# Prompt attention of a hybrid decoder step: scores over all 128 rows, value products of two heads by turns, compressed keys in one block-diagonal tile

## The chip, the cores and the metric

One core of a Trainium2 chip runs the whole program. The metric is the device time of one execution in microseconds (us), the median of the runs shown. Below, PE is TensorE's matrix engine and PEld its weight loads, DVE is VectorE, ACT is ScalarE, POOL is GpSimd; PSUM is the memory that TensorE writes, in banks of 128 rows x 512 float32 values.

## What is computed

The reference is one step of a decoder with two layers, for a prompt of 512 tokens and 8 samples of one token each, which share all weights. A layer is a feed-forward half step, three mixers side by side (a state space model, sparse attention, a short convolution) that gates merge, and a second half step. The change concerns the prompt's part of the attention mixer. There are 8 query heads in 2 groups (the kv heads), 4 queries (g) for each kv head, 64 features per head. Three branches are added with gates:

```python
s_c = jnp.einsum('btkgd,bnkd->btkgn', qg, kc)           # 31 compressed keys
p_c = masked_softmax(s_c, (c_end[None, :] <= q_pos[:, None])[None, :, None, None, :])
o_c = jnp.einsum('btkgn,bnkd->btkgd', p_c.astype(vc.dtype), vc)
...
s_s = jnp.einsum('btkgd,btknsd->btkgns', qg, ks_sel)    # selected keys
...
s_w = jnp.einsum('btkgd,bwkd->btkgw', qg, kw)           # keys of the window
...
o = g[..., 0:1] * o_c + g[..., 1:2] * o_s + g[..., 2:3] * o_w
```

With 512 prompt tokens, there are 8 blocks to select from and 16 may be selected, and the window holds 512: the selected and the window branch are both full causal attention, with keys and values of their own.

## The kernel before

Everything runs feature-major, and products are kept near float32's accuracy: a float32 operand is split into two parts, a first one (float32r) and the rest, and a product is the sum of three (lines 239 to 241 for the large projections). After the projections of queries, keys and values, the cached rows are compressed (lines 705 to 770, with the prompt's own 31 compressed keys going along with the first sample), interleaved with the samples' attention (`samples`, four pairs). The last pair's attention then runs together with `prompt_attention`: `weave` emits the two streams by turns, by the cost in ns that each step yields. Within that the scheduler of the language may still move an instruction ahead of others on its engine. After it come the state space mixer, the convolution and the gates.

`prompt_attention` works on four query tiles t of 128 tokens. Each has one unit for the compressed keys (`pa_cmp`) and eight units `pa_head`, for 2 branches (br) and 4 heads g of a group; a unit handles both kv heads. With nk = 128 (t + 1) keys, a unit of `pa_head` does, for each kv, the scores, their maximum by rows (DVE, line 1053) and the exponential (ACT, line 1054) into P; then, for each kv, `flip` transposes P in pieces of 128 (PE, line 1062) and copies it out of PSUM to PT (kv = 0 by DVE, line 1066, kv = 1 by ACT, line 1064); then `values` multiplies (PE, line 1071) and accumulates into the bank y, kv = 0 in its partitions 0 to 63 and kv = 1 in 64 to 127, that is through the two column halves of PE. At a branch's last head, the gates over the sums are brought in by four products (line 1092), DVE and POOL.

A score is the sum of three products on PE:

```python
nc.tensor.matmul(S[:, :nk], Q[:, kv, g], self.ks[:, kv, br, :nk], start=True, stop=False, ...)       # 1050
nc.tensor.matmul(S[:, :nk], Q[r, 2, g], self.ks[r, kv, br, :nk], start=False, stop=False, ...)       # 1051
nc.tensor.matmul(S[:, ts], self.identb, self.causal, start=False, stop=True, ...)                    # 1052
```

`ks[:, kv]` holds the first part of kv's keys on its own 64 rows and the second part on the other 64 (`pa_keys`); `Q[:, kv]` holds the first part of the queries twice, so line 1050 gives first by first and first by second over all 128 rows. Line 1051 adds the queries' second part by the keys' first part, on the 64 rows r of kv alone. Line 1052 adds the causal mask. `pa_queries` (lines 959 to 966) makes Q for a tile, by four ACT copies and two DVE subtractions, in a buffer named raw.

The units are emitted as a pipeline of three, two halves i each: in half 0 the first score of unit n, the first step of unit n-1 and the last of unit n-2; in half 1 the second score of unit n and the second step of unit n-1. Before, the steps of a unit are: scores kv 0; scores kv 1; flip 0; values 0 with flip 1; values 1.

`pa_cmp` has the heads in two passes, one for each kv, on 64 rows: a mask product (line 1004) and four products of 32 columns (line 1007) with the compressed keys `kcp`, then maximum, exponential and sums for all eight heads, two transposes (line 1026) and four products with the values (line 1033). The tiles P and PT of `pa_head` take the names whi and wlo of the weights' buffers that they share, and a PSUM bank is always ps.

## Time and profile before

| | |
|---|---|
| runs, median (lowest to highest) | 3239.26 us (3226.91 to 3241.25), 3 runs |
| the profiled execution, span | 3260.5 us, 62256 instructions |
| busy over the span | PE 3183.1 us (98%), PEld 3011.0 (92%), DVE 1595.2 (49%), ACT 1121.7 (34%), POOL 534.0 (16%) |
| mean granted clock of TensorE | 0.978 of full |
| prompt attention, layer 0 and layer 1 | 678 to 846 us and 2299 to 2467 us, 168 us each |

The profiled execution has no other time than its span; it lies 21 us, 0.7%, above the median of the runs. The profile's busy times are averages over stages, and a matmul's end in it is modelled: a row's duration covers the matmul's way through the engine, so consecutive rows overlap. What a product costs where TensorE is never short of work is the distance from its start to the start of the next one. Some records are missing. An fp32 product leaves two records (two passes), an fp32r or bf16 product one.

### The profile page before, as it was taken

What the parts mean: (1) busy time and instruction counts of PE and PEld (TensorE: products, weight loads), DVE (VectorE), ACT (ScalarE), POOL (GpSimd) and SP (SyncE); (2) the same over time, 40 slices, a digit from 0 to 9 for tenths busy, and PEclk for the clock granted to TensorE, in tenths of its full rate; (3) what the DMA queues carried; (4) which work ended last, traced back from release to release, by engine and by line L of the source; (5) the groups of instructions that cost most, each with busy time, mean ns of one, the idle gap of its engine ahead of it and who ended that gap; (6) DMA issues with size and microseconds to landing.
All of it is one profiled execution on the core that took longest, in us unless ns stands there. A gap on an engine that the chain in (4) does not pass through costs nothing. (4 is left out here: it accounts for less than half of the span.)

```text
span 3260.5 us, 62256 instructions
## 1 busy us (share of the span) xinstructions
PE 3183.1 (98%) x25436; PEld 3011.0 (92%) x25436; DVE 1595.2 (49%) x3590; ACT 1121.7 (34%) x2226; POOL 534.0 (16%) x807
## 2 busy tenths in 40 slices
PE   9999999999999999999999999899999999999998
PEld 8999988776899999999999999887769999999998
DVE  7633446444555455333486334455446553553334
ACT  4332225444333333332233322344443343343322
POOL 3601111211001012001147012111210010120010
PEclk9999989988999999999999999999889999999999
DMA  4543244620444332322235323445205532322321
GB/s 151 212 153 117 96 140 130 196 65 21 135 131 118 96 99 78 99 83 98 74 121 166 110 82 107 138 134 173 74 13 143 143 109 87 98 91 91 102 84 63
DMA packets 358631, 360.19 MB, mean 110 GB/s; under 512 B 40068, under 2 KB 341668, under 8 KB 358216
## 3 DMA queue, kind: packets, MB, share of 16 engines
q1 hardware_dynamic: 342584, 333.58, 32.9%
q0 software_dynamic: 7440, 20.00, 2.1%
q8 instruction: 200, 3.28, 0.4%
q10 hardware_dynamic: 8320, 2.62, 0.4%
q14 instruction: 87, 0.71, 0.1%
HBM read 332.48 MB, written 36.28 MB: 113 GB/s over the span
## 5 line engine op out<-in xcount | busy, mean ns | idle before, releaser
L239 PE MATMUL ps<-xh,whi 128*128 128x264 f32 (+1 forms) x4448 | 1259.8, 286 | 21.3 <-ACT xh L322 5.7
L240 PE MATMUL ps<-xl,whi 128*128 128x264 f32 (+1 forms) x4448 | 1260.5, 285 | 2.3 <-DVE xl L323 2.0
L241 PE MATMUL ps<-xh,wlo 128*128 128x264 f32 (+1 forms) x4448 | 1256.0, 284 | 5.5 <-issue 2.8
L239 PEld LDWEIGHTS ps<-xh,whi 128*128 128x128 f32 x4448 | 838.0, 190 | 30.3 <-ACT xh L322 7.9
L229 DVE TENSOR_TENSOR wlo<-raw,whi 128x1024 fp32r<-128x1024 f32 (+3 forms) x432 | 497.4, 1154 | 736.5 <-ACT whi L228 733.4
L240 PEld LDWEIGHTS ps<-xl,whi 128*128 128x128 f32 x4448 | 840.9, 189 | 5.4 <-DVE xl L323 3.3
L241 PEld LDWEIGHTS ps<-xh,wlo 128*128 128x128 f32 x4448 | 840.4, 189 | 5.6 <-DVE wlo L229 3.8
L228 ACT ACTIVATE whi<-raw 128x1024 fp32r<-128x1024 f32 (+2 forms) x452 | 444.4, 988 | 886.4 <-PE ps L240 774.6
L240 PE MATMUL ps<-hl,whi 128*128 128x256 f32 (+1 forms) x1408 | 398.3, 283 | 0.0
L239 PE MATMUL ps<-hh,whi 128*128 128x256 f32 (+1 forms) x1408 | 398.2, 283 | 0.0
L241 PE MATMUL ps<-hh,wlo 128*128 128x256 f32 (+1 forms) x1408 | 398.1, 283 | 0.0
L241 PEld LDWEIGHTS ps<-hh,wlo 128*128 128x128 f32 x1408 | 265.3, 188 | 0.2
L239 PEld LDWEIGHTS ps<-hh,whi 128*128 128x128 f32 x1408 | 264.8, 188 | 0.3
L240 PEld LDWEIGHTS ps<-hl,whi 128*128 128x128 f32 x1408 | 264.8, 188 | 0.1
L260 POOL TENSOR_TENSOR xf<-xf,shift 128x264 f32<-128x264 f32 (+1 forms) x84 | 79.4, 982 | 1026.2 <-ACT shift L257 1026.2
L384 DVE TENSOR_TENSOR s<-s,ps 128x264 f32<-128x264 f32 (+1 forms) x176 | 74.3, 424 | 275.9 <-PE ps L241 275.6
L708 PE MATMUL ps<-xc,whi 128*128 128x256 f32 (+1 forms) x1024 | 167.9, 297 | 1.2 <-DVE xc L694 1.2
L385 ACT ACTIVATE hh<-s 128x264 fp32r<-128x264 f32 (+1 forms) x176 | 72.7, 415 | 245.0 <-DVE s L384 244.9
L708 PEld LDWEIGHTS ps<-xc,whi 128*128 128x128 f32 x1024 | 141.3, 191 | 16.7 <-issue 9.6
L1112 POOL DMA_INDIRECT sg<-in_selT_dram,idx x96 | 92.7, 966 | 295.8 <-PE ps L1247 261.8
L1053 DVE TENSOR_REDUCE pm<-ps 128x1 f32<-128x128 f32 (+3 forms) x128 | 62.1, 488 | 111.6 <-PE ps L1052 111.2
L382 ACT ACTIVATE s<-ps 128x264 f32<-128x264 f32 (+1 forms) x176 | 66.2, 378 | 128.4 <-PE ps L241 126.2
(469 smaller groups left out, 4449.0 us busy)
## 6 DMA issues: line engine op xcount, KB each, us to landing
raw<-in_ffn_w_gu_dram SPq DMA_DIRECT2D x86, 1024.0 KB
raw<-in_w_in_dram SPq DMA_DIRECT2D x38, 1024.0 KB
raw<-in_ffn_w_down_dram SPq DMA_DIRECT2D x32, 1024.0 KB
sg<-in_selT_dram SPq DMA_DIRECT2D x160, 128.0 KB
cx<-in_cmpT_dram SPq DMA_DIRECT2D x128, 128.0 KB
raw<-in_cmpT_dram SPq DMA_DIRECT2D x128, 128.0 KB
raw<-in_ffn_w_down_dram SPq DMA_DIRECT2D x16, 768.0 KB
W<-in_winT_dram SPq DMA_DIRECT2D x16, 512.0 KB
```

Of the source, the lines that this page charges most:

```text
L228: self.copy = self.nc.scalar.activation(hi, raw, AF.Copy)
L229: self.lo.tensor_sub(lo, raw, hi.bitcast(F32))
L239: nc.tensor.matmul(o, hi[:, k], rh, start=start and k == 0, stop=False)
L240: nc.tensor.matmul(o, hi[:, k], rl, start=False, stop=False)
L241: nc.tensor.matmul(o, lo[:, k], rh, start=False, stop=stop and k == nk - 1)
L260: nc.gpsimd.tensor_sub(self.xf[:, g, a:b], self.xf[:, g, a:b], sc[:, :n])
L382: nc.scalar.activation(s[:, :n], g, AF.Silu)
L384: nc.vector.tensor_mul(s[:, :n], s[:, :n], u)
L385: nc.scalar.activation(hh[:, j, a:b], s[:, :n], AF.Copy)
L708: nc.tensor.matmul(o, w[:, 2 * qq + q2, :], x[:, 2 * q2:2 * q2 + 2, z:z + n], start=not b and s < 2 and q2 + z + m == 0, stop=s > 5 and q2 ...
L1053: nc.vector.tensor_reduce(m[:, kv:kv + 1], S[:, :nk], axis=AX.X, op=OP.max, negate=True)
L1112: nc.gpsimd.indirect_dma_start(out=t[:, k], out_offset=None, in_=flat, in_offset=bass.IndirectOffsetOnAxis(ap=self.idx[:, l, b, z, k:k + 1 ...
```

## The change

The queries' second part is now stored for each kv over all 128 rows (`Q[:, 2 + kv]`), with two subtractions more per tile, and line 1051's product runs on 128 rows like its neighbours; it thereby also adds second part by second part. `kcp` becomes a tile of two column blocks, each with one kv head's keys on its own 64 rows and zero elsewhere, and `pa_cmp` makes one pass: one mask product of 256 columns and four products of 64 columns. The heads' order in the compressed branch's tiles changes with it. `values` handles both kv in one step, each piece of 128 keys for kv 0 and then for kv 1. A unit's steps are now: scores kv 0; scores kv 1; flip 0; flip 1; values of both. Some comments are removed, which moves line numbers by a few.

```diff
-        self.kcp = a.tile([128, 32], F32, name="kcp")
+        self.kcp = a.tile([128, 2, 32], F32, name="kcp")
...
-                nc.vector.tensor_mul(self.kcp, pa[:, 384:416], self.C["kc_cos"][:, :32])
-                nc.vector.tensor_add(self.kcp, self.kcp, t)
+                nc.gpsimd.memset(self.kcp, 0.0)
+                for kv in range(2):
+                    r = slice(kv * 64, kv * 64 + 64)
+                    nc.vector.tensor_mul(self.kcp[r, kv], pa[r, 384:416], self.C["kc_cos"][r, :32])
+                    nc.vector.tensor_add(self.kcp[r, kv], self.kcp[r, kv], t[r])
...
-            nc.vector.tensor_sub(Q[own, 2], src, Q[own, kv].bitcast(F32))
+            nc.vector.tensor_sub(Q[own, 2 + kv], src, Q[own, kv].bitcast(F32))
+            nc.vector.tensor_sub(Q[other, 2 + kv], src, Q[own, kv].bitcast(F32))
...
-        for kv in range(2):
-            r = slice(kv * 64, kv * 64 + 64)
-            S = self.score_bank()
-            nc.tensor.matmul(S[:, :128], self.identb, self.cmpm[:, t, None, :].to_broadcast([128, 4, 32]), start=True,
-                             stop=False, skip_group_check=True)
-            for g in range(4):
-                nc.tensor.matmul(S[:, g * 32:g * 32 + 32], self.qT[r, g, ts], self.kcp[r], start=False, stop=g == 3,
-                                 skip_group_check=True)
...
-            if kv == 0:
-                yield 500.0
...
+        S = self.score_bank()
+        nc.tensor.matmul(S[:, :256], self.identb, self.cmpm[:, t, None, :].to_broadcast([128, 8, 32]), start=True,
+                         stop=False, skip_group_check=True)
+        for g in range(4):
+            nc.tensor.matmul(S[:, g * 64:g * 64 + 64], self.qT[:, g, ts], self.kcp, start=False, stop=g == 3,
+                             skip_group_check=True)
...
-            nc.tensor.matmul(S[:, :nk], Q[r, 2, g], self.ks[r, kv, br, :nk], start=False, stop=False, skip_group_check=True)
+            nc.tensor.matmul(S[:, :nk], Q[:, 2 + kv, g], self.ks[:, kv, br, :nk], start=False, stop=False, skip_group_check=True)
...
-        def values(kv):
-            vo = 128 + 256 * br + 64 * kv
+        def values():
             for k in range(t + 1):
-                nc.tensor.matmul(y[kv * 64:kv * 64 + 64, g, :], self.rows[:, k, vo:vo + 64], PT[:, kv, k * 128:k * 128 + 128],
-                                 start=k == 0, stop=k == t, skip_group_check=True)
+                for kv in range(2):
+                    vo = 128 + 256 * br + 64 * kv
+                    nc.tensor.matmul(y[kv * 64:kv * 64 + 64, g, :], self.rows[:, k, vo:vo + 64], PT[:, kv, k * 128:k * 128 + 128],
+                                     start=k == 0, stop=k == t, skip_group_check=True)
...
         flip(0)
         yield cost / 2
+        flip(1)
+        yield cost / 2
         if g == 0:
             self.py = self.value_bank()
         y = self.py.rearrange("p (g q) -> p g q", g=4)
-        values(0)
-        flip(1)
-        yield cost * 1.5
-        values(1)
+        values()
```

Three places show how the instructions now follow each other. The first is TensorE in t = 3 of layer 0, in the middle of the tile. Before (raw is Q, whi is P, wlo is PT; the last number is the columns, x4 that many products):

```order
L1062 MATMUL ps_9304<-cst_144,whi_9243 128x128 x4
L1071 MATMUL ps_9264<-wlo_9283,rows_4761 64x128 x4
L1050 MATMUL ps_9312<-ks_4764,raw_8954 128x512
L1051 MATMUL ps_9312<-ks_4764,raw_8954 128x512
L1052 LDWEIGHTS identb_146
L1052 MATMUL ps_9312<-masks_150,identb_146 128x128
L1062 MATMUL ps_9319<-cst_144,whi_9275 128x128 x4
L1071 MATMUL ps_9264<-wlo_9283,rows_4761 64x128 x4
```

and in the changed kernel (lines 1048 and 1049 are the two score products, 1060 the transposes):

```order
L1048 MATMUL ps_9269<-ks_4764,raw_8932 128x512
L1049 MATMUL ps_9269<-ks_4764,raw_8932 128x512
L1050 LDWEIGHTS identb_146
L1050 MATMUL ps_9269<-masks_150,identb_146 128x128
L1060 MATMUL ps_9275<-cst_144,whi_9212 128x128 x4
L1048 MATMUL ps_9283<-ks_4764,raw_8932 128x512
L1049 MATMUL ps_9283<-ks_4764,raw_8932 128x512
L1050 LDWEIGHTS identb_146
L1050 MATMUL ps_9283<-masks_150,identb_146 128x128
L1060 MATMUL ps_9290<-cst_144,whi_9245 128x128 x4
L1071 MATMUL ps_9260<-wlo_9253,rows_4761 64x128 x8
L1048 MATMUL ps_9304<-ks_4764,raw_8932 128x512
```

Before, a block of values (half a unit, four products) follows every score. Now two scores with transposes after each follow one another, and one block of eight products, of both kv, comes after the second.

The second place is ScalarE at the same time: the copies to PT (wlo; line 1064 before, 1062 now) and the exponentials (1054, 1052). Before:

```order
L1064 ACTIVATE wlo_9283<-ps_9304 128x512
L1054 ACTIVATE whi_9275,ps_8170<-ps_9294,pm_9276 128x512
L1054 ACTIVATE whi_9310,ps_8170<-ps_9312,pm_9311 128x512
L1064 ACTIVATE wlo_9318<-ps_9339 128x512
L1054 ACTIVATE whi_9310,ps_8170<-ps_9329,pm_9311 128x512
L1054 ACTIVATE whi_9345,ps_8171<-ps_9347,pm_9346 128x512
```

and now:

```order
L1062 ACTIVATE wlo_9253<-ps_9275 128x512
L1052 ACTIVATE whi_9245,ps_8173<-ps_9269,pm_9246 128x512
L1052 ACTIVATE whi_9281,ps_8173<-ps_9283,pm_9282 128x512
L1062 ACTIVATE wlo_9289<-ps_9310 128x512
L1052 ACTIVATE whi_9281,ps_8173<-ps_9304,pm_9282 128x512
```

The copy of the second transposes (wlo_9253) is taken before the exponential of the score that precedes these transposes on TensorE (ps_9269), and the values wait for that copy and, on DVE, for the first one.

The third place is TensorE at the compressed keys of t = 3. Before:

```order
L1004 LDWEIGHTS identb_146
L1004 MATMUL ps_9162<-masks_150,identb_146 128x128
L1007 MATMUL ps_9162<-kcp_4769,qT_4763 128x32
L1071 MATMUL ps_9089<-wlo_9137,rows_4761 64x128 x3
L1007 MATMUL ps_9162<-kcp_4769,qT_4763 128x32 x3
L1062 MATMUL ps_9175<-cst_144,whi_9129 128x128 x3
L1071 MATMUL ps_9089<-wlo_9137,rows_4761 64x128 x3
L1004 LDWEIGHTS identb_146
L1004 MATMUL ps_9183<-masks_150,identb_146 128x128
L1007 MATMUL ps_9183<-kcp_4769,qT_4763 128x32 x4
```

and now:

```order
L1005 LDWEIGHTS identb_146
L1005 MATMUL ps_9143<-masks_150,identb_146 128x256
L1008 MATMUL ps_9143<-kcp_4769,qT_4763 128x64 x4
L1060 MATMUL ps_9156<-cst_144,whi_9110 128x128 x3
L1071 MATMUL ps_9092<-wlo_9118,rows_4761 64x128 x6
```

Two passes of four products with 32 columns, with values and transposes in between, became one pass of four with 64.

## Rows read from the trace of the kernel before

**Rows 1.** Busy by stretch, layer 0's query tiles: us, engines, PEclk, DMA share, GB/s.

```profile
678.00:707.00 29.00, 27.74 (x177) 19.04 (x177) 16.86 (x67) 12.82 (x47) 3.35 (x4) 0.82 0.19 68
707.00:750.00 43.00, 43.00 (x287) 31.86 (x287) 17.63 (x55) 18.82 (x59) 5.07 (x9) 0.92 0.11 26
750.00:795.00 45.00, 45.00 (x225) 30.92 (x223) 17.24 (x40) 17.72 (x48) 4.62 (x4) 0.77 0.00 1
795.00:846.00 51.00, 50.64 (x329) 36.31 (x329) 24.25 (x46) 22.48 (x52) 4.63 (x4) 1.00 0.11 32
```

**Rows 2.** Timeline, one half-unit of t = 3: start us, us, engine, line, operation.

```profile
817.05 0.50 PE L1050 MATMUL ps<-ks,raw 128*128 128x512 f32 x1
...
817.48 0.18 PEld L1051 LDWEIGHTS ps<-ks,raw 64*128 64x128 f32 x1 [0.25 <-issue]
...
817.90 0.23 PE L1052 MATMUL ps<-masks,identb 128*128 128x128 bf16 x1
...
817.97 0.61 PE L1062 MATMUL ps<-cst,whi 128*128 128x128 f32 x4
818.17 0.69 DVE L1053 TENSOR_REDUCE pm<-ps 128x1 f32<-128x512 f32 x1 [1.12 <-PE ps L1052]
...
818.51 1.09 PE L1071 MATMUL ps<-wlo,rows 128*64 128x128 f32 x8
818.61 0.60 ACT L1064 ACTIVATE wlo<-ps 128x512 f32<-128x512 f32 x1 [1.35 <-PE ps L1062]
819.11 0.68 ACT L1054 ACTIVATE whi<-ps,pm 128x512 f32<-128x512 f32 x1
...
819.52 0.49 PE L1050 MATMUL ps<-ks,raw 128*128 128x512 f32 x1
```

**Rows 3.** Timeline, PE, products of the projection after layer 1's stage.

```profile
2469.17 0.28 PE L241 MATMUL ps<-xh,wlo 128*128 128x264 f32 x1
2469.29 0.28 PE L239 MATMUL ps<-xh,whi 128*128 128x264 f32 x1
```

**Rows 4.** Timeline, PE, start of the stage: compressed keys, then scores of t = 0.

```profile
680.13 0.23 PE L1004 MATMUL ps<-masks,identb 128*128 128x128 bf16 x1
680.29 1.07 PE L1007 MATMUL ps<-kcp,qT 64*128 64x32 f32 x8
681.29 0.33 PE L1050 MATMUL ps<-ks,raw 128*128 128x128 f32 x1
681.55 0.32 PE L1051 MATMUL ps<-ks,raw 64*128 64x128 f32 x1
```

**Rows 5.** Timeline, PE: column halves by turns (two places), then on one half.

```profile
678.62 0.44 PE L736 MATMUL ps<-hc,w 128*64 128x128 f32 x4
678.88 0.39 PE L736 MATMUL ps<-hc,w2r 128*64 128x128 f32 x4
679.20 0.66 PE L740 MATMUL ps<-w,hc 128*128 128x64 f32 x4
...
703.53 0.44 PE L1071 MATMUL ps<-wlo,rows 128*64 128x128 f32 x4 [0.16 <-DVE pw L1096]
703.90 0.32 PE L1051 MATMUL ps<-ks,raw 64*128 64x128 f32 x1
...
704.93 0.43 PE L1071 MATMUL ps<-wlo,rows 128*64 128x128 f32 x2
705.29 0.23 PE L1052 MATMUL ps<-masks,identb 128*128 128x128 bf16 x1
```

**Rows 6.** Busy by stretch at the low clock, and timeline around it, PE.

```profile
753.60:774.10 20.50, 20.50 (x67) 13.39 (x65) 8.26 (x23) 7.30 (x21) 2.31 (x2) 0.50 0.00 1
...
751.48 0.85 PE L1007 MATMUL ps<-kcp,qT 64*128 64x32 f32 x6
...
764.21 0.67 PE L1050 MATMUL ps<-ks,raw 128*128 128x384 f32 x1
764.81 0.69 PE L1051 MATMUL ps<-ks,raw 64*128 64x384 f32 x1
```

More of the change, by code (lines that the diff above doesn't have):

```diff
@@ L724, in second @@
                     r = 2 if i else 1
-                    t = p0.tile([128, 2, r, 32], F32, name=f"ph{i}")
+                    t = p0.tile([128, r, 2, 32], F32, name=f"ph{i}")
                     nc.vector.memset(t, 0.0)
-                    nc.scalar.activation(t[:, :, :, :31], hv[:, :, None, 130:161].to_broadcast([128, 2, r, 31]),
+                    nc.scalar.activation(t[:, :, :, :31], hv[:, None, :, 130:161].to_broadcast([128, r, 2, 31]),
                                          AF.Gelu_apprx_tanh, bias=self.hpe[:, i:i + 1])
@@ L737, in second @@
                     if b == 0:
-                        nc.tensor.matmul(pa[r, 384 + j * 32:416 + j * 32], w, hp[0][:, kv, 0], start=True, stop=True)
+                        nc.tensor.matmul(pa[r, 384 + j * 32:416 + j * 32], w, hp[0][:, 0, kv], start=True, stop=True)
             for kv in range(2):
@@ L748, in second @@
                 nc.vector.tensor_mul(t, pa[:, 416:448], self.C["kc_sin"][:, :32])
-                nc.vector.tensor_mul(self.kcp, pa[:, 384:416], self.C["kc_cos"][:, :32])
-                nc.vector.tensor_add(self.kcp, self.kcp, t)
+                nc.gpsimd.memset(self.kcp, 0.0)
[3 more added lines that the diff above has]
+                    nc.vector.tensor_add(self.kcp[r, kv], self.kcp[r, kv], t[r])
                 pv = self.bank(self.saM)
-                nc.tensor.matmul(pv[:, :64], hp[1].rearrange("p k r n -> p (k r n)"), self.w2[:, 1], start=True, stop=True)
+                nc.tensor.matmul(pv[:, :64], hp[1].rearrange("p r k n -> p (r k n)"), self.w2[:, 1], start=True, stop=True)
                 nc.gpsimd.memset(self.vcp, 0.0)
@@ L755, in second @@
                     ks = slice(k * 32, k * 32 + 32)
-                    nc.vector.tensor_copy(self.vcp[ks, k % 2::2, k // 2], pv[ks, None, :64].to_broadcast([32, 2, 64]))
+                    nc.vector.tensor_copy(self.vcp[ks, k // 2::2, k % 2], pv[ks, None, :64].to_broadcast([32, 2, 64]))
             yield 1300.0
@@ L1016, in pa_cmp @@
-        nc.scalar.activation(P8, P8, AF.Exp)
-        nc.vector.tensor_reduce(m8[:, 1], P8, axis=AX.X, op=OP.add)
-        nc.vector.tensor_scalar(m8[:, 1], m8[:, 1], 1e-30, None, op0=OP.max)
-        nc.vector.reciprocal(m8[:, 2], m8[:, 1])
-        gt = self.gtok[:, t].rearrange("p (k a b r) -> p r a k b", k=2, a=2, r=3)
-        nc.vector.tensor_mul(m[:, 3], m[:, 2], gt[:, 0])
-        nc.vector.tensor_mul(P8, P8, m8[:, 3, :, None].to_broadcast([128, 8, 32]))
-        yield 500.0
+        P, m = p.tile([128, 8, 32], F32, name="cP"), p.tile([128, 4, 8], F32, name="cm")
@@ new lines, in pa_cmp @@
+        S = self.score_bank()
[4 more added lines that the diff above has]
+                             skip_group_check=True)
+        s3 = S[:, :256].rearrange("p (h n) -> p h n", n=32)
+        nc.vector.tensor_reduce(m[:, 0], s3, axis=AX.X, op=OP.max)
@@ new lines, in pa_cmp @@
+        nc.vector.tensor_scalar(m[:, 0], m[:, 0], BIG / 4, None, op0=OP.max)
+        nc.vector.tensor_sub(P, s3, m[:, 0, :, None].to_broadcast([128, 8, 32]))
+        yield 900.0
+        nc.scalar.activation(P, P, AF.Exp)
+        nc.vector.tensor_reduce(m[:, 1], P, axis=AX.X, op=OP.add)
+        nc.vector.tensor_scalar(m[:, 1], m[:, 1], 1e-30, None, op0=OP.max)
+        nc.vector.reciprocal(m[:, 2], m[:, 1])
+        gt = self.gtok[:, t].rearrange("p (k g r) -> p r g k", k=2, r=3)
+        nc.vector.tensor_mul(m[:, 3].rearrange("p (g k) -> p g k", k=2), m[:, 2].rearrange("p (g k) -> p g k", k=2), gt[:, 0])
@@ L1024, in pa_cmp @@
+        nc.vector.tensor_mul(P, P, m[:, 3, :, None].to_broadcast([128, 8, 32]))
+        yield 0.0
         T = self.bank(self.saT)
         for a in range(2):
-            nc.tensor.transpose(T[:, a * 128:a * 128 + 128], P8[:, a * 4:a * 4 + 4, :], self.ident)
+            nc.tensor.transpose(T[:, a * 128:a * 128 + 128], P[:, a * 4:a * 4 + 4, :], self.ident)
         PT = p.tile([128, 2, 128], F32, name="cPT")
@@ L1029, in pa_cmp @@
         yield 220.0
+        yield 0.0
         Y = self.value_bank()
@@ L1035, in pa_cmp @@
         yield 950.0
-        yield 0.0
     def pa_head(self, t, g, br, p, s):
@@ L1047, in pa_head @@
         for kv in range(2):
-            r = slice(kv * 64, kv * 64 + 64)
             S = self.score_bank()
             nc.tensor.matmul(S[:, :nk], Q[:, kv, g], self.ks[:, kv, br, :nk], start=True, stop=False, skip_group_check=True)
-            nc.tensor.matmul(S[:, :nk], Q[r, 2, g], self.ks[r, kv, br, :nk], start=False, stop=False, skip_group_check=True)
+            nc.tensor.matmul(S[:, :nk], Q[:, 2 + kv, g], self.ks[:, kv, br, :nk], start=False, stop=False, skip_group_check=True)
             nc.tensor.matmul(S[:, ts], self.identb, self.causal, start=False, stop=True, skip_group_check=True)
```

7 lines of the change are left out of this document (removed).

## The prediction

> **What bounds the kernel now.** I read the busy time by stretch first. The change sits in the prompt's attention, one stage per layer; in layer 0 it runs from 678 to 846 us, cut in [rows 1] at the four query tiles (t = 0 to 3). PE is busy nearly the whole of each tile, VectorE at most 16.86 of 29 us and ScalarE 12.82 of 29 in t = 0, under half of either in t = 3. So the stage goes as TensorE goes, and what matters is how TensorE's time is made up. Second, the timeline of one half-unit (one head, one branch, one kv) of t = 3 [rows 2]: two score products of 512 columns start 0.43 and 0.42 us apart (817.05, 817.48, 817.90), the causal mask takes 0.07, four transposes 0.54 (817.97 to 818.51), eight records of values 1.01 (818.51 to 819.52): 2.47 together, with TensorE never waiting for another engine. But before the 64-row product's weight load the load path sat idle for 0.25 us with nothing to wait for: the engine drains when a product on 64 rows follows one on 128. Where the rows don't change, products of 264 columns start 0.12 us apart [rows 3], that is 0.23 for 512 columns.
>
> **Scores on all 128 rows.** The second product (L1051) ran on 64 rows, after one and before one on 128; both switches go. Today's price is 0.26 at 128 columns (681.29 to 681.55 in [rows 4]) and 0.43 at 512 [rows 2]; in between, 0.32 and 0.37. The slope, 0.17 for 384 columns, is 0.057 per 128; so 512 columns without a switch cost 0.23, as [rows 3] also gives. 384 cost 0.17. For 256 and 128 I take 0.12, the start-to-start time of [rows 3], as a floor; 0.06 is the other end for 128 columns. Saved per product: 0.14, 0.20, 0.20, 0.20 us for t = 0 to 3. There are two per half-unit, and 4 heads x 2 branches x 2 kv x 2 layers = 32 half-units per tile: 9.0 + 12.8 + 12.8 + 12.8 = 47.4 us. The product now also multiplies the rows that were left out, at no price: a column takes as long on 64 rows as on 128 (0.42 beside 0.43).
>
> **Values by turns.** Today a kv head's values are one block on one column half: 0.36 us for two records in t = 0 (704.93 to 705.29, [rows 5]), 1.01 for eight in t = 3 [rows 2], so 0.58 and 0.80 in between. The changed kernel puts both heads into one block whose steps alternate between the halves. The same kernel shows what that does: four records on L1071 that fall on both halves take 0.37 us (703.53 to 703.90), no more than two on one half; and the compression's L736, of the same shape and written by turns, runs eight records in 0.58 us (678.62 to 679.20, all in [rows 5]), where one half needs 1.01 [rows 2]. So one block for both, as long as one is today. Saved per head and branch: 0.36, 0.58, 0.80, 1.01; 16 of these per tile over both layers: 5.8 + 9.3 + 12.8 + 16.2 = 44.1 us. The bounds are 0 and 44. One switch into the halves per head goes too; that can't be told from the transposes in [rows 2], so 0, and at most 0.1 x 64 = 6.
>
> The Trainium skill's page "TensorE: Matmul & The Clock Gate" speaks against this term: Part 3, under what overlaps and what doesn't, lets a weight load run beside a product in flight only if it goes to other rows of the array. The two halves share all rows, so by it the records would go singly and this term would be 0. The L736 row and the four-record L1071 row disagree with it, and I go by them.
>
> **Compressed keys block-diagonal.** Today a unit has twice a mask and eight records on 64 rows with 32 columns, 1.16 us each time (680.13 to 681.29, [rows 4]). Afterwards there is one mask and eight records of 64 columns on 128 rows. That costs between half of 1.16 and 1.16; I take 1.16, since the records stand 0.125 apart with only 32 columns in them, so columns don't set their pace. Saved: 1.16 x 8 units = 9.3 us.
>
> **What is added, and its cover.** Two more subtractions per tile for the queries' second part on VectorE, and four small operations instead of two plus a memset for the keys, in a layer's compression. VectorE has 12 us free in t = 0 and 27 in t = 3 [rows 1]; cost 0. If that cover were gone, the eight subtractions per layer would stand on the path with some 0.7 us each, as long as a copy of 512 columns today (0.69 for the reduction of 512 in [rows 2]): 11 us in all. The values of a head now wait for both copies of transposed probabilities, and the second is ScalarE's. In the changed order of ScalarE that copy stands ahead of the exponential of the later scores, so it runs when its transposes end: by [rows 2] 0.64 us after their start (817.97 to 818.61), 0.60 long, so 1.24. TensorE's work from those transposes to the values is 0.54 + 0.53 + 0.54 = 1.61 us in t = 3. That covers it; in t = 0 the same sums shrink to some 0.7 on both sides, which leaves no slack.
>
> **The sum.** Per tile, both layers: t = 0: 9.0 + 5.8 + 2.3 = 17.1; t = 1: 24.4; t = 2: 27.9; t = 3: 31.3; together 100.7 us. In t = 0 and t = 1 chains through VectorE and ScalarE are nearly as long as TensorE's work, and the last samples' attention, whose steps wait for each other, runs there. I give up half of t = 0 and a quarter of t = 1: 8.5 + 6.1 = 14.6, leaving 86.
>
> Then TensorE's clock. From 753.6 to 774.1 the granted clock is 0.50, the lower of the two levels, and it fell after the narrow score records of the compressed keys (six of them from 751.48) [rows 6]. Two products of 384 columns then start 0.60 apart (764.21 to 764.81), 1.6 times the 0.37 of the full level. This stretch thus costs 20.5 x (1 - 1/1.6) = 7.7 us per layer, 15 in all. The narrow records halve. Whether that is enough can't be read from the trace (0 to 15); I take half, 8. So 86 + 8 = **94 us** less: 3260.5 - 94 = 3166.5 for the profiled execution's span. That span is 21 us over the median of the runs; taken from the median, 3239.3 - 94 = **3145 us**.
>
> **Rivals.** (a) Everything works and nothing is lost: 100.7 + 15 + 6 = 122 us, 3117. For it: TensorE hardly waits today (27.74 of 29 us busy in t = 0, all of t = 1 and t = 2, [rows 1]). Against: t = 0 has no slack. (b) The values' new wait bites. If the copy ran behind the exponential of the scores before it, in t = 3 it would take 0.27 us from the mask to the reduction, 0.69 for that, 0.68 for the exponential, 0.60 for the copy [rows 2]: 2.24, against 0.07 + 1.61 of TensorE's work: 0.56 us per head, for all 64 heads 36. Gain 58: 3181. It decides where ScalarE takes the exponential first; the order shows it the other way round, but that is an order and not a time. (c) The change doesn't do what it says: the halves don't run side by side over long blocks. Then 47.4 + 9.3 - 9.4 + 8 = 55: 3184. The L736 row speaks against it. (d) Slower: TensorE's clock stays at the lower level. With drains and half the value blocks gone, transposes fill more of the stage (0.54 of 2.47 us per half-unit now, of about 1.6 then). If the engine is held at 1.2 GHz throughout, a stage of 168 us that shrinks by 43 + 8 to 117 costs 1.6 times that, 187: 19 more per layer, 3278 us. It breaks even with three quarters of the stage at the lower level; around there the time stays the same. Against it: in t = 3 the clock is 1.00 with these transposes in [rows 1], and the narrow records, after which it fell, become fewer.
>
> The same page's Part 4 says that the full clock does not engage for transposes. By that (d) would come about; no stretch of transposes alone is long enough here to show it.
>
> **Chances.** Forecast 0.61, (a) 0.15, (b) 0.12, (c) 0.06, (d) 0.03, its break-even 0.03. A measurement of this kernel can tell about 0.5%, 16 us, from no change. Faster: the first four, 0.94; same 0.03; slower 0.03. The forecast alone spans 3125 to 3165; the range takes in (a) with the lower end for narrow score products (0.06 x 64 = 4 us more) and up to (b): 3110 to 3192.
>
> **What would show it.** Right: no idle load path around the second score product, and starts 0.23 us apart in t = 3; sixteen value records in about 1.0 us; t = 3 some 16 us shorter per layer and t = 0 some 4 to 8; a head of t = 3 in 3.2 us instead of 4.94. Wrong: value records waiting for ScalarE's copy (b), sixteen records in 2 us (c), a granted clock below 0.7 over the stage (d), or stages as long as now with TensorE idle in t = 0 and t = 1, which would mean that the chains through VectorE and ScalarE bound more than I gave up.

## The result, and the profile after the change

The changed kernel takes **3147.8 us** (median of 4 runs, 3143.2 to 3151.4), the kernel before, in the same session, 3233.3 (4 runs, 3226.9 to 3241.3): a ratio of 0.9737, with a 95% interval of 0.9717 to 0.9757, so some 85 us less. The forecast was 3145, its range 3110 to 3192.

The page of the changed kernel, span and first line of busy times. TensorE was busy for 3183.1 us before, with 72 records more:

```profile
span 3149.7 us, 62116 instructions
PE 3078.8 (98%) x25364; PEld 2949.6 (94%) x25364; DVE 1599.2 (51%) x3586; ACT 1121.1 (36%) x2226; POOL 531.5 (17%) x809
```

To compare whole stages, one cut serves all kernels: from the last product on L708 (the compression, which the change leaves alone) to the first product of the projection behind the stage (L239). Busy time by stretch; the columns are those of [rows 1], and the last three are granted clock, DMA share and GB/s. Before, layer 0 and layer 1:

```profile
675.80:845.70 169.90, 168.23 (x1026) 119.48 (x1025) 77.03 (x211) 73.65 (x207) 19.47 (x22) 0.89 0.10 30
2297.10:2467.00 169.90, 168.22 (x1027) 119.47 (x1026) 77.02 (x211) 73.64 (x207) 19.46 (x22) 0.89 0.10 29
```

After:

```profile
665.10:788.70 123.60, 119.00 (x992) 89.61 (x990) 78.85 (x205) 72.63 (x207) 18.92 (x22) 0.97 0.14 40
2231.90:2355.50 123.60, 119.03 (x992) 89.64 (x990) 78.61 (x205) 72.63 (x207) 18.92 (x22) 0.97 0.14 41
```

A stage is 46.3 us shorter, both 92.6. TensorE's busy time in it fell by more, 49.2 us: it now waits 4.6 us per stage, where it waited 1.7. The other engines have nearly the same work. And the mean granted clock rose from 0.89 to 0.97.

The two profiled spans differ by 110.8 us, the medians by 85.5. The other 18 us of the spans lie outside the two stages (7.8 of them in the first 496 us, 6.0 between layer 0's stage and layer 1's projection), mostly in code that the change leaves alone: the profiled execution of the kernel before was a long one, over 20 us above the median. Stage lengths below each come from one profile, and the times are what decides.

The stage by query tile, cut at each tile's first score product. Before (layer 0; t = 0, 1, 2, 3):

```profile
678.10:710.40 32.30, 31.04 (x198) 21.88 (x198) 18.11 (x72) 15.37 (x56) 4.30 (x4) 0.82 0.17 60
710.40:754.50 44.10, 44.10 (x295) 32.45 (x295) 18.00 (x56) 18.57 (x54) 4.41 (x9) 0.93 0.11 26
754.50:800.20 45.70, 45.70 (x234) 31.72 (x234) 17.56 (x41) 16.37 (x45) 5.29 (x5) 0.79 0.04 12
800.20:845.70 45.50, 45.14 (x288) 31.70 (x287) 22.32 (x40) 21.43 (x49) 3.59 (x3) 1.00 0.08 23
```

After, the lines that answer to [rows 1]:

```profile
665.90:693.30 27.40, 24.80 (x189) 18.55 (x188) 19.76 (x71) 15.64 (x56) 4.09 (x4) 0.88 0.24 76
693.30:728.20 34.90, 34.22 (x282) 26.09 (x282) 18.91 (x57) 17.72 (x55) 5.07 (x9) 1.00 0.13 32
728.20:757.20 29.00, 28.01 (x233) 20.92 (x232) 19.34 (x43) 17.60 (x48) 4.75 (x5) 1.00 0.05 14
757.20:788.70 31.50, 31.18 (x290) 23.59 (x288) 20.84 (x37) 21.24 (x49) 4.51 (x4) 1.00 0.13 35
```

So t = 0 to 3 are 4.9, 9.2, 16.7 and 14.0 us shorter. Only t = 0 still has a low clock; TensorE waits there for 2.6 of 27.4 us.

One whole head of t = 3 after the change, timeline of PE (start us, busy us, line, operation), which answers to [rows 2]:

```profile
772.01 0.50 PE L1048 MATMUL ps<-ks,raw 128*128 128x512 f32 x1
772.35 0.40 PE L1049 MATMUL ps<-ks,raw 128*128 128x512 f32 x1
772.58 0.23 PE L1050 MATMUL ps<-masks,identb 128*128 128x128 bf16 x1
772.65 0.61 PE L1060 MATMUL ps<-cst,whi 128*128 128x128 f32 x4
773.02 0.48 PE L1048 MATMUL ps<-ks,raw 128*128 128x512 f32 x1
773.33 0.39 PE L1049 MATMUL ps<-ks,raw 128*128 128x512 f32 x1
773.56 0.23 PE L1050 MATMUL ps<-masks,identb 128*128 128x128 bf16 x1
773.63 0.61 PE L1060 MATMUL ps<-cst,whi 128*128 128x128 f32 x4
774.16 1.09 PE L1071 MATMUL ps<-wlo,rows 128*64 128x128 f32 x16
775.19 0.38 PE L1091 MATMUL ps<-cst,pc 128*128 128x128 f32 x1
```

The head takes 3.18 us, where two half-units took 4.94. Sixteen records of values, by turns on the two column halves, need 1.03 us (774.16 to 775.19), as long as eight on one half did. The second score product now starts its successor after 0.23 us (772.35 to 772.58, 773.33 to 773.56), where it took 0.42. But the first product still holds 0.31 to 0.34 (773.02 to 773.33, 772.01 to 772.35) and not 0.23. The load path in the same half-unit suggests why (PEld, start us, busy us):

```profile
772.60 0.42 PEld L1060 LDWEIGHTS ps<-cst,whi 128*128 128x128 f32 x4
772.99 0.19 PEld L1048 LDWEIGHTS ps<-ks,raw 128*128 128x128 f32 x1
773.10 0.19 PEld L1049 LDWEIGHTS ps<-ks,raw 128*128 128x128 f32 x1
```

The first product's weights begin to load at 772.99, 0.03 us before it starts, because the load path has the four transposes' weights until then. In the stream of 264 columns a load begins some 0.12 us ahead of its product (kernel before):

```profile
99.97 0.19 PEld L239 LDWEIGHTS ps<-xh,whi 128*128 128x128 f32 x1
...
100.09 0.28 PE L239 MATMUL ps<-xh,whi 128*128 128x264 f32 x1
```

The load thus has 0.09 us less of a start, and 0.31 is 0.08 more than 0.23. That is read from rows; it was not tried by itself.

Values now wait for both copies. The line L1071 with what ended TensorE's waits for it, over the whole run:

```profile
L1071 PE MATMUL ps<-wlo,rows 128*64 128x128 f32 x640 | 60.4, 284 | 1.5 <-ACT wlo L1062 0.6 <-DVE wlo L1064 0.4
```

### The profile page after: what moved, and what is told of

The parts are those of the page before. It is cut to its first block, busy times and chain, and to the rows that moved or that the text cites. A ratio compares the mean times of both kernels' runs of the same rounds, so it can differ in the third digit from the quotient of the medians.

```text
span 3149.7 us, 62116 instructions
## 1 busy us (share of the span) xinstructions
PE 3078.8 (98%) x25364; PEld 2949.6 (94%) x25364; DVE 1599.2 (51%) x3586; ACT 1121.1 (36%) x2226; POOL 531.5 (17%) x809
## 5 line engine op out<-in xcount | busy, mean ns | idle before, releaser
L239 PE MATMUL ps<-xh,whi 128*128 128x264 f32 (+1 forms) x4448 | 1257.5, 285 | 15.3 <-ACT whi L228 7.8
L239 PEld LDWEIGHTS ps<-xh,whi 128*128 128x128 f32 x4448 | 837.0, 189 | 20.1 <-ACT whi L228 8.8
L239 PE MATMUL ps<-hh,whi 128*128 128x256 f32 (+1 forms) x1408 | 398.2, 283 | 0.0
L239 PEld LDWEIGHTS ps<-hh,whi 128*128 128x128 f32 x1408 | 264.9, 188 | 0.3
L708 PE MATMUL ps<-xc,whi 128*128 128x256 f32 (+1 forms) x1024 | 165.2, 295 | 0.0
L708 PEld LDWEIGHTS ps<-xc,whi 128*128 128x128 f32 x1024 | 140.1, 190 | 14.6 <-issue 8.5
L386 DVE TENSOR_TENSOR hl<-s,hh 128x264 fp32r<-128x264 f32 (+1 forms) x176 | 76.6, 437 | 33.5 <-ACT hh L385 33.5
```

Source lines behind the costliest of these rows:

```text
L239: nc.tensor.matmul(o, hi[:, k], rh, start=start and k == 0, stop=False)
L386: nc.vector.tensor_sub(hl[:, j, a:b], s[:, :n], hh[:, j, a:b].bitcast(F32))
L708: nc.tensor.matmul(o, w[:, 2 * qq + q2, :], x[:, 2 * q2:2 * q2 + 2, z:z + n], start=not b and s < 2 and q2 + z + m == 0, stop=s > 5 and q2 ...
```

## The experiments

Twelve runs in three sessions, each beside the kernel before on the same chip. Every ratio is to the kernel before, and a difference in us is that of the ratios, times the 3233 us of the kernel before; with their intervals such a difference is good to some 5 to 12 us. "Stage" is both layers' stages together by the cut above: 339.8 us before, 247.2 after.

### One part alone

**scores_only**: the kernel before, with the queries' second part on all 128 rows.

```diff
-            nc.vector.tensor_sub(Q[own, 2], src, Q[own, kv].bitcast(F32))
+            nc.vector.tensor_sub(Q[own, 2 + kv], src, Q[own, kv].bitcast(F32))
+            nc.vector.tensor_sub(Q[other, 2 + kv], src, Q[own, kv].bitcast(F32))
...
-            nc.tensor.matmul(S[:, :nk], Q[r, 2, g], self.ks[r, kv, br, :nk], start=False, stop=False, skip_group_check=True)
+            nc.tensor.matmul(S[:, :nk], Q[:, 2 + kv, g], self.ks[:, kv, br, :nk], start=False, stop=False, skip_group_check=True)
```

> The kernel before, with the second score product on all 128 rows and nothing else of the change. Theory (each switch between 64 and 128 rows drains TensorE): the score products of t = 3 start 0.23 us apart instead of 0.43, the term of 47 us less what t = 0 and t = 1 cannot use (8), so about 3233 - 40 = 3193 us; the clock still falls at the compressed keys. Rival (the drain is hidden, since the values or the transposes behind it would wait anyway): within 5 us of 3233.

Measured: 3222.4 us, ratio 0.9914 (0.9882 to 0.9945), 28 us less; stage 302.6. It lies between the two, and well under the forecast's term of 47.

**values_only**: the kernel before, with one block of values per head whose steps alternate between the halves.

```diff
-        def values(kv):
-            vo = 128 + 256 * br + 64 * kv
+        def values():
...
+                for kv in range(2):
+                    vo = 128 + 256 * br + 64 * kv
...
+        flip(1)
+        yield cost / 2
...
-        values(0)
-        flip(1)
-        yield cost * 1.5
-        values(1)
+        values()
```

> The kernel before, with the values of both kv heads in one step, by turns, and nothing else of the change. Theory (the column halves run side by side): eight records become sixteen in the same 1.0 us, 44 us less what t = 0 and t = 1 cannot use (5): about 3233 - 39 = 3194 us. Rival (the halves share the array's rows, so the records go one by one): only the second switch into the halves is saved, 6 us or less, 3227 to 3233.

Measured: 3219.8 us, ratio 0.9901 (0.9864 to 0.9937), 32 us less; stage 302.1. Between the two. The clock gives nothing to it: in this kernel's profile the stages are at 0.50 for 34.1 and 37.5 us, about as long as before (37.5), only mostly earlier, in t = 0 and around the start of t = 1.

**cmp_only**: the kernel before, with the block-diagonal compressed keys.

```diff
-        self.kcp = a.tile([128, 32], F32, name="kcp")
+        self.kcp = a.tile([128, 2, 32], F32, name="kcp")
...
-                nc.tensor.matmul(S[:, g * 32:g * 32 + 32], self.qT[r, g, ts], self.kcp[r], start=False, stop=g == 3,
...
+            nc.tensor.matmul(S[:, g * 64:g * 64 + 64], self.qT[:, g, ts], self.kcp, start=False, stop=g == 3,
```

> The kernel before, with the compressed keys block-diagonal and one pass over them, and nothing else of the change. Theory (the two narrow passes make the clock fall, at 709 and 754 us in the trace of before): the stage's stretches at the lower level after the second and third tile's compressed keys are gone, 9 us for the pass itself and up to 15 to 20 for the clock: 3206 to 3212. Rival (the clock falls for the drains of the scores and of the value blocks): the stretches stay, 9 us alone: 3224.

Measured: 3236.0 us, ratio 0.9965 (0.9948 to 0.9982), 11 us less; stage 317.1. That is about the forecast's price of the passes alone, but part of it is the clock: in the median its runs' granted clock is 0.984, that of the kernel before beside it 0.981, and in its profile the stages are at 0.50 for 13.7 and 17.1 us. The low stretch in t = 2 is gone, as the theory said; one layer has a new one of 10.2 us in t = 1.

### One part undone

The three alone make 28 + 32 + 11 = 71 us, less than the 85 of the whole (the stages, against the one long profile of the kernel before, make 98 where the whole makes 92.6); so each was also taken out of the changed kernel, by the same lines in reverse.

**no_scores** (the second product on 64 rows again):

> The changed kernel with the second score product on 64 rows again. Theory 1 (the terms add): the two switches come back at each of 256 products, S2 to the mask 0.43 instead of 0.23 us in t = 3: 3148 + 47 = 3195 us, less up to 7 for what t = 0 and t = 1 hide: 3188 to 3195. Rival (the parts are worth less together than alone, since the same waits are removed twice): alone this part gave 28 us of 3249, so 3176 us or less.

Measured: 3174.5 us, ratio 0.9820 (0.9789 to 0.9850), so 0.0083 or 27 us above the changed kernel's; stage 271.6, 24.4 more. The rival's number, though not for its reason: alone and undone the part is worth the same, 27 to 28. The term was too large. The timeline of t = 3 in this kernel (PE):

```profile
779.85 0.48 PE L1048 MATMUL ps<-ks,raw 128*128 128x512 f32 x1
780.26 0.50 PE L1049 MATMUL ps<-ks,raw 64*128 64x512 f32 x1
780.69 0.23 PE L1050 MATMUL ps<-masks,identb 128*128 128x128 bf16 x1
```

Going back to 64 rows costs 0.20 on the second product (0.43 against 0.23) but only 0.10 on the first (0.41 against 0.31).

**no_values** (a block of values per kv head again):

> The changed kernel with one block of values per kv head again, each on one column half. Theory 1 (the terms add): eight records 1.01 us twice in t = 3 where the changed kernel needs 1.03 for sixteen: 3148 + 44 = 3192 us, less up to 7 for what t = 0 and t = 1 hide: 3185 to 3192. Rival (values by turns also bring the wait for ScalarE's copy, so undoing them gives something back): alone this part gave 32 us of 3249, so 3180 us or less; then the changed kernel's records of values would wait for that copy in t = 0 and t = 1.

Measured: 3186.2 us, ratio 0.9857 (0.9830 to 0.9884), 39 us above the changed kernel's; stage 285.7, 38.5 more. That is in theory 1's range, near its lower end: the term was nearly right, and no wait shows that gives something back.

**no_cmp** (two masks and eight narrow records on 64 rows again):

> The changed kernel with the compressed keys as they were (two masks and eight records on 64 rows per unit). The passes themselves cost 1.16 us more for each of 8 units, 9 us. Theory 1 (the narrow records are what TensorE's clock falls after): the low stretch behind t = 2's compressed keys comes back, 20 us at 0.50 in each layer's stage beside the 7 us that the changed kernel has there, worth some 8 us a layer: 3148 + 9 + 16 = 3173 us, the stage 13 us longer per layer. Rival (the clock falls for other reasons, and the narrow records have nothing to do with it): 3157 us, the stage 4 to 5 us longer per layer, low time in it as in the changed kernel.

Measured: 3167.0 us, ratio 0.9788 (0.9758 to 0.9818), 16 us above; stage 261.6, 14.4 more. Halfway between the theories, and the place of the low clock is neither's: 20.5 us of each stage are at 0.50, in t = 0 and t = 1, and none behind t = 2's compressed keys, where theory 1 had put it. That is 13.7 us more per layer than in the changed kernel, and at the forecast's price, 0.375 us for each, some 10 of the 14.4. In this kernel's busy time by stretch the second of the low stretches and all that follows it:

```profile
700.00:706.80 6.80, 6.80 (x30) 5.49 (x30) 2.85 (x10) 3.80 (x12) 0.86 (x1) 0.50 0.00 0
706.80:798.80 92.00, 90.58 (x785) 68.34 (x784) 56.61 (x129) 52.66 (x140) 13.27 (x16) 1.00 0.11 29
```

Undone, the parts sum to 27 + 39 + 16 = 82 us in the times, 77.3 in the stages: the whole of the 85 in the times, within the intervals.

### Is it the alternation?

**values_blocks**: the changed kernel, but all records of kv 0 and then all of kv 1 in the same step.

```diff
-            for k in range(t + 1):
-                for kv in range(2):
-                    vo = 128 + 256 * br + 64 * kv
+            for kv in range(2):
+                vo = 128 + 256 * br + 64 * kv
+                for k in range(t + 1):
```

> The changed kernel, with the values of both heads still in one step, but all of kv 0 and then all of kv 1. Theory 1 (pairs form only where the order alternates): the blocks go one after the other, sixteen records in 1.9 us in t = 3, about 38 us more than the changed kernel's 3148, so 3186. Theory 2 (TensorE starts a later record of the other half ahead of its turn, so that it is enough that the two blocks stand next to each other): sixteen records in 1.0 us, 3145 to 3153.

Measured: 3185.0 us, ratio 0.9794 (0.9762 to 0.9827); stage 255.1, 7.9 more than the changed kernel's. The records give a number between the two theories, 1.51 us for sixteen (timeline of PE, t = 3):

```profile
787.86 1.58 PE L1071 MATMUL ps<-wlo,rows 128*64 128x128 f32 x16
789.37 0.60 PE L1091 MATMUL ps<-cst,pc 128*128 128x128 f32 x3
```

The first four records start singly, some 0.11 us apart, then two start in each 0.109 us, and the last four go singly again. A record doesn't say which half it is on; but records of one half go singly (eight in 1.01), so this pace fits TensorE starting records of the other half ahead of their turn, and only some of them. So writing them by turns is worth having. The time in us agrees with theory 1, but on this chip the kernel before also stood at 3248.5 us, 15 more than in the other sessions; by the ratios the kernel is 18 us above the changed one, and the stage and the rows are the better witnesses.

### What the clock falls after

The forecast had put the low clock down to the narrow score records of the compressed keys, since it fell behind them. Two kernels try that in the changed kernel, whose records are 64 columns on 128 rows and no longer 32 on 64.

**cmp_none** (the eight records left out, so that those scores are the mask alone):

```diff
-        for g in range(4):
-            nc.tensor.matmul(S[:, g * 64:g * 64 + 64], self.qT[:, g, ts], self.kcp, start=False, stop=g == 3,
-                             skip_group_check=True)
...
```

> The changed kernel without the eight score records of the compressed keys: their scores are the mask alone, the products with the keys are left out. In the changed kernel a unit's records take some 0.9 us, so 4 us less per layer by the work. Theory 1 (the clock falls after these narrow records): the one fall in the stage, 6.8 us behind t = 0's compressed keys, is gone too, 0 us at the lower clock in the stage, 3.6 + 2.6 = 6 us less per layer. Rival (t = 0 is where TensorE waits most, and the clock falls for that): the fall stays, 7 to 10 us long, and the stage is 4 us shorter or less.

Measured: 3140.2 us, ratio 0.9711 (0.9685 to 0.9738); stage 238.5, 8.5 less than the changed kernel in the same session. The fall stays without the records, 6.8 us in layer 0 and 10.2 in layer 1. Layer 0's busy time by stretch, ahead of the fall and in it:

```profile
665.00:672.50 7.50, 5.31 (x44) 4.14 (x42) 6.96 (x24) 5.47 (x17) 1.87 (x2) 1.00 0.84 277
672.50:679.30 6.80, 5.97 (x33) 5.40 (x33) 4.20 (x21) 3.01 (x12) 1.04 (x1) 0.50 0.02 5
```

**cmp_twice** (the records issued twice, and a small mask behind):

```diff
-        for g in range(4):
+        for g in (0, 1, 2, 3, 0, 1, 2, 3):
...
```

> The changed kernel with the eight score records of the compressed keys issued twice (their scores are doubled), and a small mask behind them. 0.9 us more work per unit, 4 us per layer. Theory 1 (the clock falls after these narrow records): longer or more falls behind the compressed keys, 20 us or more at the lower clock in each layer's stage, so 4 + 5 = 9 us more per layer, 3166 us. Rival (the clock falls for waits in t = 0, not for these records): 6.8 us at the lower clock as now, 4 us more per layer, 3156 us.

Measured: 3155.0 us, ratio 0.9768 (0.9739 to 0.9796); stage 253.4, 6.4 more than the changed kernel in the same session. One fall per stage again, 10.2 us in t = 0, and the clock is full from there on:

```profile
670.60:680.80 10.20, 10.16 (x52) 8.43 (x51) 6.64 (x31) 5.47 (x25) 1.04 (x1) 0.50 0.05 20
...
680.80:789.20 108.40, 105.27 (x920) 79.76 (x920) 66.95 (x156) 62.13 (x171) 15.59 (x18) 1.00 0.09 24
```

Theory 1 falls in both, for the changed kernel's records: with twice the records in t = 1 to 3 too, no fall comes there. Ahead of the fall in t = 0 TensorE was busy for only 5.31 of 7.5 us in cmp_none, and for 5.94 of 7.3 in the changed kernel; that speaks for the rival. But waits can't be all of it, since in the kernel before the fall in t = 0 comes behind a stretch without any (5.96 of 6.00 us busy from 672 to 678, and then):

```profile
678.00:682.00 4.00, 4.00 (x31) 3.09 (x31) 2.36 (x9) 1.33 (x3) 1.04 (x2) 0.99 0.87 283
682.00:692.20 10.20, 9.13 (x44) 6.95 (x42) 5.46 (x28) 5.02 (x21) 0.00 (x0) 0.50 0.20 79
```

The same holds for no_cmp (busy for 3.83 of 3.87 us ahead of it) and for the fall that the forecast priced, the one in t = 2 [rows 6]. That one is gone in every profile with the changed values or the changed compressed keys (cmp_only, no_cmp, no_values; values_only and no_scores but for 3.4 us in one layer), and there, 10 us long, in scores_only. So the old records don't make it by themselves: no_cmp and values_only still have them. The fall around the start of t = 1 is there in the kernel before, scores_only, values_only, no_cmp and one layer of cmp_only.

Over the whole stage there is a clear line all the same. The profiles of the four kernels with the old compressed keys show 20.5 to 37.5 us per layer at 0.50 (before 37.5, values_only 34.1 and 37.5, scores_only 23.9, no_cmp 20.5), and the ten other profiles 6.8 to 17.1. So the low clock goes with the old compressed keys, two passes of 32 columns on 64 rows, among other things; cmp_none and cmp_twice, which have no such pass, don't test that. What in them does it stays open.

### A further step: values of two heads in one block

The switch into and out of the column halves shows in the rows: ahead of the first record of a block (774.16 in the changed kernel) and ahead of the product behind the block (775.19), the load path sits idle for 0.17 us, waiting for nothing that the profile shows. **two_heads** holds back every second head's values for one round and issues both heads' together.

```diff
...
                 if old is not None and i == 0:
-                    c += next(old)
+                    hold.append(old)
+                    if (n - 2) % 9 % 2 == 0:
+                        c += sum(next(h) for h in hold)
+                        hold = []
...
```

> The changed kernel with the values of two heads in one block of 32 records in t = 3 (every second head's values wait one head longer). Theory 1 (a switch into and out of the column halves costs TensorE 0.09 us each way, 0.203 instead of 0.109 between records): 32 blocks fewer in both layers, 0.19 each: 6 us, 3142 us; t = 3 some 0.7 us shorter per layer, too little for the times to tell, so it is read from the stage: 121.2 instead of 122.75. Rival (the time of a switch is a cost of the first weight load, or the held head delays the chains through VectorE and ScalarE in t = 0): the stage as long as now or longer, 3148 to 3156.

Measured: 3141.5 us, ratio 0.9709 (0.9683 to 0.9736); stage 239.4. A block of 32 records takes 1.90 us, 0.16 less than two of 16 (timeline of PE):

```profile
772.43 1.97 PE L1074 MATMUL ps<-wlo,rows 128*64 128x128 f32 x32
774.33 0.94 PE L1094 MATMUL ps<-cst,pc 128*128 128x128 f32 x6
```

By this cut t = 3 is only 0.2 us shorter, and most of the gain lies in t = 1 and t = 2 (by stretch, t = 0 to 3, against the four lines of the changed kernel above):

```profile
668.30:695.20 26.90, 25.29 (x187) 19.33 (x185) 19.31 (x70) 15.21 (x54) 4.10 (x4) 0.81 0.23 78
695.20:729.00 33.80, 33.32 (x284) 25.80 (x283) 18.69 (x55) 17.67 (x57) 5.05 (x9) 1.00 0.12 30
729.00:756.10 27.10, 26.06 (x221) 19.83 (x219) 18.29 (x41) 17.59 (x49) 4.62 (x4) 1.00 0.03 7
756.10:787.40 31.30, 30.98 (x304) 24.45 (x302) 21.38 (x41) 20.75 (x50) 4.63 (x4) 1.00 0.14 41
```

Part of that is the cut: the values of a held head come one head later, so t = 3 has 152 records of values between its cuts, where it had 140, and t = 2 has 88 for 98. With a pair in 0.109 us, twelve records are worth some 0.65 us (an estimate), so on the same work t = 3 is some 0.85 us shorter, near the 0.7 of theory 1. The gain is in the values' own time: over the four tiles of layer 0 TensorE is busy with them for 26.2 us, where it was for 30.2. Why t = 1 and t = 2 gain more than the forecast gave them stays open. A switch can cost more than one per block, as the changed kernel's t = 2 shows, where three of the eight blocks are torn, two records ahead and ten behind another product (PE):

```profile
738.80 0.43 PE L1071 MATMUL ps<-wlo,rows 128*64 128x128 f32 x2
739.16 0.45 PE L1049 MATMUL ps<-ks,raw 128*128 128x384 f32 x1
739.53 0.87 PE L1071 MATMUL ps<-wlo,rows 128*64 128x128 f32 x10
740.34 0.87 PE L1060 MATMUL ps<-cst,whi 128*128 128x128 f32 x6
```

That is 0.36 + 0.81 us, where a whole block of twelve takes 0.80 (756.09 to 756.89). But blocks of two_heads are torn in t = 2 as well (2, 4 and 18 records, 6 and 18). Since 119.8 could have been the draw of one execution, both kernels ran again, side by side.

**after_again**: no edit to the changed kernel.

> The changed kernel as it is, as the yardstick on this chip: 3148 us within 0.4%, 6.8 us at the lower clock in each layer's stage, the stage 123.5 us from the last product ahead of it.

Measured: 3145.5 us (3141.8 to 3148.9), ratio 0.9729 (0.9705 to 0.9753); stage 247.0.

**two_heads_again**: the same kernel as two_heads.

> The kernel with the values of two heads in one block, again, beside the changed kernel on the same chip. In one profile its stage was 3.7 us shorter per layer. Theory 1: that is what the change is worth, 7 us of 3148 (0.2%), and the stage comes out at 119 to 120 us again. Rival: 119.8 was the draw of one execution, and the stage is 122 to 124 us.

Measured: 3140.5 us (3133.3 to 3142.8), ratio 0.9708 (0.9684 to 0.9733); stage 239.5, against 239.4 the first time. Busy by stretch, both layers' stages:

```profile
667.30:787.20 119.90, 116.32 (x992) 89.90 (x990) 77.78 (x205) 71.64 (x207) 18.87 (x22) 0.96 0.14 41
2224.90:2344.50 119.60, 115.26 (x992) 88.52 (x990) 77.52 (x205) 71.61 (x207) 18.89 (x22) 0.97 0.14 41
```

The stage is 3.7 us shorter per layer in four stages out of four, so theory 1 holds for the size, and for t = 3 once the cut is allowed for. The medians, 5 us apart, go the same way, but the intervals of the two ratios overlap: the times alone don't show it.

## Why the prediction was right, and where it was not

The time was right to 3 us, the gain, 94 against 85, to 9. Part of that is luck: the terms of the work were too large together by some 33 us, and the discount for waits and a clock worth twice the forecast offset most of it.

**The bound** holds. TensorE was the stage's limit and still is (119.0 of 123.6 us busy), and TensorE's own time is what the change cut.

**Scores, 47.4 us, measured 28 alone and 24 to 27 undone.** This is the step that failed. "Today's price" was taken for both switches, "saved per product: 0.14, 0.20, 0.20, 0.20", and "there are two per half-unit". For the second product that came true: the median from its start to the mask's fell from 0.26 to 0.12, 0.31 to 0.12, 0.37 to 0.18 and 0.42 to 0.23 us in t = 0 to 3 (against no_scores in t = 2, where the kernel before was at the low clock). But the first product saves only 0.075, 0.09, 0.09 and 0.095 (no_scores against the changed kernel): it stands behind transposes or values, and by the rows its weight load, which begins 0.03 us ahead of it, stays exposed. The price of the row switch and that of the load had been read as one. By these sizes the term is 32 x (0.21 + 0.28 + 0.28 + 0.29) = 34 us, of which t = 0 to 2 hide some: per layer, t = 3 of no_scores is 4.4 us longer, of 4.6 by these sizes, and t = 2, in the layer without a fall, 1.6 of 4.5. What could have shown it ahead of time is a row of the kernel before that [rows 2] leaves out, the load of the first product, 0.01 us ahead of it though the rows of the array don't change there:

```profile
817.04 0.19 PEld L1050 LDWEIGHTS ps<-ks,raw 128*128 128x128 f32 x1 [0.17 <-issue]
```

Only the load of the second product was looked at.

**Values by turns, 44.1 us, measured 32 alone and 38 to 39 undone.** The mechanism held, and so did the sizes taken from the other rows: sixteen records in 1.03 us for a forecast of about 1.0, and a whole block of t = 2 in 0.80 for 0.80. The torn blocks of t = 2 make up a part of what is missing. Rival (c) is out with that. The sentence in Part 3 of the Trainium skill's page "TensorE: Matmul & The Clock Gate" by which weight loads run beside a product only on other rows, taken alone, would have made this term 0. Every one of these records uses all 128 rows, and they go in pairs, so the measurement decides against it here.

**Compressed keys, 9.3 us, measured 11 alone and 14 to 16 undone, clock included.** One mask and eight records of 64 columns on 128 rows take 0.95 us in the changed kernel, for a forecast of 1.16 at the upper end:

```profile
726.54 0.27 PE L1005 MATMUL ps<-masks,identb 128*128 128x256 bf16 x1
726.65 1.00 PE L1008 MATMUL ps<-kcp,qT 128*128 128x64 f32 x8
727.49 0.39 PE L1060 MATMUL ps<-cst,whi 128*128 128x128 f32 x2
```

In no_cmp each of the two passes takes 1.15 (735.01 to 736.16). The pace is that of records and not of columns, as forecast. But without the clock (below) the term is worth only some 4 or 5 us.

**The cover.** Rival (b)'s wait hardly exists: 0.6 us in the whole run for ScalarE's copy, where it was priced at 36, since the copy runs ahead of the exponentials, as the order had it (in the head above from 773.30, the next exponential from 773.79). No wait of TensorE for the subtractions on VectorE shows. Against the 14.6 us given up for t = 0 and t = 1, TensorE's new waiting there is 4.0 us over both layers, with some 2 more in t = 2 (4.6 us per stage for 1.7); t = 0 and t = 1 came out at 4.9 and 9.2 us less per layer, which is what the sum had for them after the discount, 4.3 and 9.2; but in both there was less low clock than before, which the forecast had not counted there.

**The clock, 8 us.** Right in that it mattered, half the size, and open in why. In the two profiles the stage's time at 0.50 fell from 37.5 to 6.8 us per layer; by the forecast's own ratio of 1.6 that is 30.7 x 0.375 = 11.5 us per layer, 23 in all. But this is one long execution of the kernel before. The granted clock of the single runs gives the usual amount: 0.981 in the median for the kernel before, in each of the three sessions, and 0.987 to 0.988 for the changed kernel. A mean of 0.981 is 3.8% of the run at 0.50, some 123 us, and the changed kernel has 75 to 79. The price holds in the times too: in one session the kernel before took 3239.4 and 3240.2 us at 0.979 and 0.978, and 3224.7 and 3229.2 at 0.984, 13 us for some 36 us less at 0.50. So by estimate some 17 of the 85 us are the clock's, and 68 the work's. The same estimate takes 7 off the 11 of cmp_only, 11 off the 16 of no_cmp (0.983), 2 each off the 27 of no_scores and the 39 of no_values, nothing off the 28 of scores_only (0.981), and adds 4 to values_only (0.978 to 0.982): the work is 28 + 36 + 4 = 68 alone and 25 + 37 + 5 = 67 undone, closer than the intervals warrant.

That the narrow records cause the falls by themselves does not hold: the fall in t = 2 is gone in no_cmp with the old records in place, and the one in t = 0 stays without any (cmp_none). That they have a part in it is not excluded. Rival (d) is out: the clock is 1.00 from t = 1 on, with transposes taking 0.90 of the 3.18 us of a head in t = 3. What the Trainium skill's page "TensorE: Matmul & The Clock Gate" says in Part 4, that the full clock does not engage for transposes, did not bring the clock down here, where the transposes stand among other products.

So 47 + 44 + 9 - 15 + 8 was forecast. By the parts undone, without the clock, the scores were some 22 too large, the values 7 and the compressed keys 4: 33 in all, of which the 15 given up for waits took off about half; and the clock gave some 17 for 8. The forecast was not off by more because the discount for waits and a clock priced at half covered a mistake that had nothing to do with either.

## What to carry over

A product on a part of the rows costs TensorE time on either side (here 0.20 us behind it and 0.10 ahead of it, at 512 columns); where its other rows can be filled with something useful or with zeros, do that. But price each side by itself: look at the load path ahead of each of the products, since a load that was late before the change will still be late after it. Products on half the columns want to be written by turns, in long unbroken blocks: alternation halved their time, and merging two heads' blocks gave another 3.7 us per stage.

When a fall of the clock follows an operation, that is no proof that the operation caused it; leave the operation out and look again, in the kernel in which it fell. And the granted clock of every run, not of one profile, tells what share of a gain is the clock's.

## What the runs showed that was not expected

- Products written in blocks per column half still overlap in part: sixteen records in 1.51 us, between the 1.03 by turns and the 2.0 one half after the other. By that pace TensorE takes records of the other half out of turn, a few at a time.
- Going into the column halves and out again costs a fixed time per block: 32 records in one block take 1.90 us, two blocks of 16 take 2.06.
- Two passes of compressed keys of 1.15 us where the changed kernel has one of 0.95 left t = 2 as long as it was (29.0 us in no_cmp and in the changed kernel). TensorE's waits don't take up the difference (0.9 and 1.0 us in that tile), but the order of work moves with the passes: in no_cmp one block of values is torn there and not three, and the values' records keep TensorE busy for 8.6 us instead of 9.4.
